# A hybrid attention and convolution block on eight cores: a rewrite of the whole kernel around 128-token interleaving, stationary P^T and merged stages

## The chip, the cores and the metric

The kernel runs on all 8 NeuronCores of one Trainium2 chip, two dies of four cores. The metric is the device time of the slowest core in microseconds. Engines are named as in the profile: PE is TensorE's matmul, PEld its weight load, DVE is VectorE, ACT is ScalarE, POOL is GpSimd, SP is SyncE. SP and POOL only issue DMAs here, apart from some POOL operations (the largest, in before, are eight of 2.4 us).

This program has a slower state that comes and goes: one die's cores, or both dies', show a lower granted TensorE clock and the run is some per cent longer. Before ran in 1544.24, 1740.64, 1663.52 and 1546.27 us; the first and last are fast runs. A ratio is the mean time of one kernel's fast runs over the mean of the other's fast runs of the same rounds, so it is not quite the ratio of the medians quoted beside it.

## The reference, cut to what matters

```python
D_MODEL, BATCH, SEQ = 1024, 4, 4096          # 4 differential heads, two 64-wide maps each, v of 128
xn = rmsnorm(x, norm_mix_g)
u = xn @ w_in                                # 5120 columns: conv b, c, v; q, k, v; two gates
y_a = (b_g * causal_conv3(c_g * v_a)) @ w_a_out
p = softmax(q k^T / 8 + alibi, causal)       # (B, H, 2, q, k)
o = (p[:, :, 0] - lam * p[:, :, 1]) @ v
y_b = (rmsnorm(o, subln_g) * (1 - lam_init)) @ w_b_out
x = x + (sigmoid(gate_a) * y_a + sigmoid(gate_b) * y_b) @ w_o
h = rmsnorm(x, norm_mlp_g) @ w_mlp_in        # 1024 -> 4096
x = x + square(relu(h)) @ w_mlp_out
return rmsnorm(x, norm_final_g)
```

Two cores share one batch element. Each owns half of its 4096 tokens and computes K and V for all of them.

## The kernel before

A core owns four blocks of 512 tokens. There are four stages, with a barrier of all engines between them: projections, attention, gates and output projection, MLP. In the first stage, normalising is done with tokens on partitions, where the scale is one number per partition, and the result is transposed on TensorE:

```python
S.op("act", lambda e: e.activation(xb[:ntok], xt[:ntok], AF.Square, accum_out=st[:ntok, 0:1]), ...)
... Ln, then Exp with scale -0.5: the reciprocal root ...
S.op("dve", lambda e: e.tensor_scalar_mul(xb[:ntok], xt[:ntok], st[:ntok, 2:3]), ...)
for c in range(8):
    S.op("pe", lambda e, c=c: e.transpose(pst[:, c, :ntok], xb[:ntok, c * 128:(c + 1) * 128], ...), ...)
S.op("dve", lambda e: e.tensor_tensor(dst, pst[:, :, :ntok], gcols...to_broadcast(...), ALU.mult), ...)
```

Attention keeps V stationary and streams P (keys on partitions, 512 queries). A second set of matmuls with an all-ones weight gives the row sums:

```python
mm(Ops[:, m, cs:512], Vt[:, kt, h * 128:(h + 1) * 128], PT[:, m, cs:512], ...)    # emit_pv
mm(Lps[:, m, cs:512], ones_bf, PT[:, m, cs:512], ...)                             # emit_lsum
```

In the MLP, W1 and W2 come in eight groups, each group's output is added to x in SBUF.

The softmax here doesn't subtract the row's maximum and nothing guards it: scores larger than these inputs give would overflow.

## Time and profile before

The page of the profiled run of before, slowest core. The first two lines are the span and each engine's busy time; the digits are tenths, in 40 equal slices, of PE busy, granted clock and DMA; the last line is the chain of work that ended last, by engine.

```profile
span 1546.6 us, 22141 instructions; the slowest of 8 cores (1531.8 to 1546.6 us)
...
PE 1376.5 (89%) x6824; PEld 584.5 (38%) x6824; DVE 709.2 (46%) x963; ACT 712.6 (46%) x1066; POOL 67.5 (4%) x72
...
PE   1989999878999999999367888897999999999995
...
PEclk9999999989999999999788999999999999999998
DMA  8861100330000000000197254443331313121105
...
PE 77%; DVE 8%; DMA 5%; ACT 5%; issue 3%; SPq 0%; POOL 0%; POOLq 0%; DVEq 0%; ACTq 0%
```

TensorE is busy 89% of the time and 77% of the last chain. The holes are at the start, around slice 19 (the hand-over from attention to gates) and at the very end. The table by stretches of the same core says what they are worth (columns: stretch, its length, then busy us and instruction count of each engine, clock, DMA share, GB/s):

```profile
core 7: us, PE busy (x) PEld busy (x) DVE busy (x) ACT busy (x) POOL busy (x), PEclk, DMA share, GB/s
0.00:65.00 65.00, 29.95 (x177) 15.84 (x178) 20.57 (x41) 21.02 (x48) 5.29 (x13) 1.00 0.80 161
...
362.00:760.00 398.00, 374.80 (x1888) 129.69 (x1886) 157.06 (x89) 309.93 (x308) 0.00 (x0) 0.99 0.00 1
760.00:820.00 60.00, 31.42 (x109) 11.51 (x108) 10.11 (x18) 21.25 (x39) 7.01 (x8) 0.73 0.97 201
820.00:1081.60 261.60, 223.81 (x1142) 104.40 (x1141) 126.80 (x195) 138.91 (x267) 22.80 (x27) 0.95 0.44 59
1081.60:1546.60 465.00, 445.65 (x2048) 200.19 (x2048) 240.63 (x408) 109.95 (x200) 30.01 (x22) 0.98 0.25 51
```

One step of attention, from the timeline of before in order of time (start us, duration us, engine, line; the x2 is a pair of 64-row QK matmuls, one in each half of the array's rows):

```profile
599.84 1.04 PE L348 MATMUL ps_all<-big 128*128 128x512 bf16 x4
600.01 1.11 ACT L675 ACTIVATE big<-ps_all,big 128x1024 bf16<-128x1024 f32 x1 [0.18 <-PE ps_all L350]
...
600.81 0.39 PE L350 MATMUL ps_all<-big 64*128 64x512 bf16 x2
...
601.13 1.04 PE L348 MATMUL ps_all<-big 128*128 128x512 bf16 x4
```

A step takes 1.29 us (599.84 to 601.13): four 512-column matmuls and a QK pair on TensorE, one 1.11 us exp on ACT. Attention is bound by TensorE, closely followed by the exps.

### The profile page before, as it was taken

The page shows a single profiled execution, that of the slowest core. Times are in us where ns is not written, and L with a number is a line of the kernel's source. Part 1 is how long each engine was busy: PE and PEld are TensorE (multiplying, and loading weights), DVE is VectorE, ACT ScalarE, POOL GpSimd, SP SyncE. Part 2 cuts the span into 40 slices and gives each one's busy share as a digit, 9 for nine tenths or more (in the row PEclk, how much of TensorE's full clock was granted, in tenths as well). Part 3 has the DMA queues.
Part 4 walks back from the last instruction along what each step waited for, and adds up shares of the span by engine and source line. Part 5 has one row for each costly group of instructions (what it writes and reads, how often), then busy time and mean ns, then how long its engine had stood idle before and what let it go on. Part 6 is the DMA issues. An engine that isn't in the chain of part 4 may idle for free.

```text
span 1546.6 us, 22141 instructions; the slowest of 8 cores (1531.8 to 1546.6 us)
## 1 busy us (share of the span) xinstructions
PE 1376.5 (89%) x6824; PEld 584.5 (38%) x6824; DVE 709.2 (46%) x963; ACT 712.6 (46%) x1066; POOL 67.5 (4%) x72
## 2 busy tenths in 40 slices
PE   1989999878999999999367888897999999999995
PEld 0444444323333333333123434343444444444441
DVE  2444454476553332333323454455253563564476
ACT  2553322356778878888244555463312112102217
POOL 0000000000000000000000000000000000000004
PEclk9999999989999999999788999999999999999998
DMA  8861100330000000000197254443331313121105
GB/s 163 182 159 53 44 28 1 54 56 1 1 1 1 1 1 1 1 0 1 19 259 103 36 74 53 57 56 55 53 57 31 53 29 55 28 32 25 28 11 208
DMA packets 63907, 80.06 MB, mean 52 GB/s; under 512 B 2984, under 2 KB 48168, under 8 KB 63792
## 3 DMA queue, kind: packets, MB, share of 16 engines
q0 software_dynamic: 53120, 44.04, 20.2%
q1 hardware_dynamic: 10672, 34.60, 7.0%
q8 instruction: 58, 0.95, 0.2%
q14 instruction: 57, 0.47, 0.1%
HBM read 114.29 MB, written 8.39 MB: 79 GB/s over the span
## 4 chain that ended last, share of the span: by engine, by line
PE 77%; DVE 8%; DMA 5%; ACT 5%; issue 3%; SPq 0%; POOL 0%; POOLq 0%; DVEq 0%; ACTq 0%
PE ps_all L348 70%; PE ps_all L350 6%; DMA big<-w_in 3%; DMA big<-xs 2%; DVE big L706 2%; DVE big L700 1%; DVE big L809 1%; ACT big L675 1%; ACT big L962 1%; ACT big L790 1%; PE ps_all L387 1%; PE ps_all L807 1%; ACT big L973 1%; DVE big L856 0%; DVE big L390 0%
## 5 line engine op out<-in xcount | busy, mean ns | idle before, releaser
L348 PE MATMUL ps_all<-big 128*128 128x512 bf16 (+3 forms) x5600 | 1270.6, 378 | 98.9 <-ACT big L834 24.4
L348 PEld LDWEIGHTS ps_all<-big 128*128 128x128 bf16 x5600 | 517.4, 100 | 741.2 <-issue 212.1
L675 ACT ACTIVATE big<-ps_all,big 128x1024 bf16<-128x1024 f32 (+1 forms) x320 | 329.1, 1049 | 101.2 <-PE ps_all L350 68.0
L997 ACT ACTIVATE big<-ps_all 128x512 bf16<-128x512 f32 x128 | 76.4, 597 | 319.1 <-PE ps_all L348 319.1
L1011 DVE TENSOR_TENSOR big<-ps_all,big 128x512 f32<-128x512 f32 x256 | 175.7, 690 | 39.3 <-PE ps_all L348 36.1
L350 PE MATMUL ps_all<-big 64*128 64x512 bf16 (+3 forms) x736 | 130.0, 350 | 11.6 <-ACT big L675 6.9
L998 DVE TENSOR_TENSOR big<-big 128x512 bf16<-128x512 bf16 x128 | 54.4, 425 | 175.9 <-ACT big L997 175.9
L706 DVE RECIPROCAL big<-big 128x1024 f32<-128x1024 f32 x16 | 104.8, 6552 | 2.0 <-DVE big L705 0.5
L700 DVE COPY big<-ps_all 128x1024 f32<-128x1024 f32 x16 | 19.6, 1222 | 175.5 <-PE ps_all L348 175.5
L350 PEld LDWEIGHTS ps_all<-big 64*128 64x128 bf16 x736 | 36.1, 93 | 147.6 <-issue 141.3
L850 DVE TENSOR_TENSOR big<-ps_all,big 128x512 f32<-128x512 f32 x32 | 22.1, 691 | 143.7 <-PE ps_all L348 94.1
L790 ACT ACTIVATE big<-big 128x1024 bf16<-128x1024 f32 x28 | 29.6, 1056 | 96.9 <-DVE big L789 91.3
L366 ACT ACTIVATE big<-big 128x1024 bf16<-128x1024 f32 (+1 forms) x33 | 34.9, 1058 | 56.9 <-DVE big L488 26.2
L319 POOL DMA_DIRECT2D big<-w_in x34 | 29.9, 883 | 710.3 <-DVE big L725 469.3
L387 PE MATMUL ps_all<-big 128*128 128x128 bf16 (+1 forms) x264 | 21.5, 228 | 39.4 <-DVE big L365 31.0
L376 DVE TENSOR_SCALAR big<-big 128x1024 bf16<-128x1024 f32 (+1 forms) x33 | 25.0, 759 | 53.1 <-ACT big L370 53.1
L390 DVE TENSOR_TENSOR big<-ps_all,big 128x1024 bf16<-128x1024 bf16 (+1 forms) x33 | 39.1, 1186 | 3.4 <-PE ps_all L387 3.3
L705 DVE COPY big<-ps_all 128x1024 f32<-128x1024 f32 x16 | 19.6, 1224 | 41.5 <-PE ps_all L348 41.4
L401 DVE CAST big<-ps_all 128x512 bf16<-128x512 f32 x24 | 16.5, 688 | 43.0 <-PE ps_all L348 43.0
L387 PEld LDWEIGHTS ps_all<-big 128*128 128x128 bf16 (+1 forms) x264 | 18.2, 102 | 47.1 <-issue 40.9
L725 DVE SCALAR_TENSOR_TENSOR big<-big 128x512 bf16<-128x512 f32 x16 | 12.0, 750 | 50.5 <-ACT big L724 50.5
L834 ACT ACTIVATE big<-ps_all,big 128x512 f32<-128x512 f32 x32 | 21.7, 679 | 27.3 <-PE ps_all L348 27.3
(67 smaller groups left out, 558.9 us busy)
## 6 DMA issues: line engine op xcount, KB each, us to landing
big<-xs SPq DMA_DIRECT2D x48, 512.0 KB, 7.8
big<-w_in POOLq DMA_DIRECT2D x32, 512.0 KB, 6.8
big<-w POOLq DMA_DIRECT2D x16, 1024.0 KB, 8.7
out<-big SPq DMA_DIRECT2D x16, 512.0 KB, 2.9
big<-w_in POOLq DMA_DIRECT2D x4, 1024.0 KB, 33.3
big<-w_in POOLq DMA_DIRECT2D x1, 2048.0 KB, 25.0
big<-w_o POOLq DMA_DIRECT2D x1, 2048.0 KB, 29.0
big<-w_a POOLq DMA_DIRECT2D x1, 1024.0 KB, 12.1
```

What stands on the lines that cost most here:

```text
L348: S.op("pe", lambda e: e.matmul(out, lhsT, rhs, start=start, stop=stop), reads=reads, writes=writes)
L350: S.op("pe", lambda e: e.matmul(out, lhsT, rhs, start=start, stop=stop, tile_position=tp), reads=reads, writes=writes)
L366: S.op("act", lambda e: e.activation(xb[:ntok], xt[:ntok], AF.Square, accum_out=st[:ntok, 0:1]), reads=[xkey, skey], writes=[xbkey, skey])
L387: S.op("pe", lambda e, c=c: e.transpose(pst[:, c, :ntok], xb[:ntok, c * 128:(c + 1) * 128], ident[:ntok, :ntok]), reads=[xbkey, "ident"], ...
L390: S.op("dve", lambda e: e.tensor_tensor(dst, pst[:, :, :ntok], gcols.unsqueeze(2).to_broadcast([128, 8, ntok]), ALU.mult), reads=[pkey, gk ...
L675: S.op("act", lambda e: e.activation(PT[:, :, cs:512], Sps[:, buf, :, cs:512], AF.Exp, bias=btab[:, bidx:bidx + 1], scale=0.125), reads=[" ...
L700: S.op("dve", lambda e: e.tensor_copy(c["Ocp"], Ops), reads=["O"], writes=[c["k"] + "O"])
L706: S.op("dve", lambda e: e.reciprocal(c["Lcp"], c["Lcp"]), reads=[k + "L"], writes=[k + "L"])
L790: S.op("act", lambda e: e.activation(xb, xt, AF.Square, accum_out=st[:, 0:1]), reads=[xkey, skey], writes=[xbkey, skey])
L997: S.op("act", lambda e, r=r, ph=ph: e.activation(r, ph, AF.Relu), reads=[phk], writes=[rk])
L998: S.op("dve", lambda e, r=r, fc=fc, sl=sl: e.tensor_tensor(hb[:, fc, sl * 512:(sl + 1) * 512], r, r, ALU.mult), reads=[rk], writes=["h2_%d ...
L1011: S.op("dve", lambda e, T=T, half=half, pz=pz: e.tensor_tensor(x_mid[:, T, half * 512:(half + 1) * 512], pz, x_mid[:, T, half * 512:(half ...
```

## The change: its intent and its core

The rewrite changes nearly every line; what matters of it is this.

1. Tokens are owned in interleaved tiles of 128, so that both cores' causal triangles are trimmed at 128 tokens.
2. P^T is the stationary operand and V the moving one, with a column of ones in V: one matmul gives 128 outputs and the row sum.
3. Attention is merged with projections of later blocks and with gates: between the halves of an attention step stand "chunks" of 4 or 8 matmuls, which all use one PSUM bank.
4. x arrives already transposed, so nothing of it is transposed on TensorE. But then a token's scale is needed along the free dimension, on all partitions. The kernel computes it with tokens on partitions from a second copy of x, writes the 512 numbers to DRAM and reads them back broadcast.
5. Intermediates (normalised x, branch inputs, residual x) are spilled to DRAM, and W1 and W2 stay resident in the MLP. The barriers are gone.

```diff
-            mm(Ops[:, m, cs:512], Vt[:, kt, h * 128:(h + 1) * 128], PT[:, m, cs:512], st["first"], st["last"],
-            mm(Lps[:, m, cs:512], ones_bf, PT[:, m, cs:512], st["first"], st["last"],
+                mm(oview(m, t), PT.ap[:, m, t * 128:(t + 1) * 128], v.ap[:, h, 0:129], start,
+                   p["last"] and s == 1, [PT, v], [pk(OB[(m, t)][0])], skip=True)
...
+    def stat_tile(blk, t, xt):
+        act(lambda e: e.activation(junk.ap, xt.ap, AF.Square, accum_out=ss1[blk].ap[:, t:t + 1]), ...)
+    def row_bcast(blk, src, dst, n, p):
+        row = rr_sp[blk, 0:n]                                   # in DRAM
+        ... dma_start(out=row.rearrange("(t p) -> p t", p=128), in_=src.ap[:, 0:4])
+        ld(dst.ap, ... rr_sp[blk:blk + 1, 0:n].partition_broadcast(128), [dst], [key])
...
+        def nrm(c):                                             # 8 of these per block, on DVE
+            dve(lambda e, k=k: e.scalar_tensor_tensor(x[k].ap, x[k].ap, ccol(C_GMIX + k), R_b.ap, ...))
...
+    def merged(g, upto, ratio):
+        oring[0] = Ring([7])                                    # one PSUM bank for all chunks
+        for slot in attn(g):
+            run_deferred()
+            credit += ratio / 2.0
+            while credit >= 1.0: ... one_chunk()
+        run_deferred(True)      # (called after it)
...
+    m_w1()                      # all of W1 and a quarter of W2, issued at once after attention
+    until(...)                  # the last two gate groups
+    m_load(0)                   # the first MLP block's input
```

## The prediction

> All times are for the fast state. (Before ran in 1544 to 1741 us; its profile, both dies near clock 0.96, took 1546.6.)
>
> What bounds before. The page shows PE busy 89% and 77% of the chain that ended last: TensorE, with holes. In the raw matmul records, back-to-back starts are 216 ns apart for 512 columns, 56 ns for 128 columns with a new weight each time (transposes), and a row-tiled QK pair adds about 420 ns between 512-column matmuls (312 before it, 322 to the next, less 216). With the built program's counts, before needs about 1324 us of warm PE. The other 222 us are holes: the table by stretches shows PE busy 30 of the first 65 us (DMA share 0.80), 57 of 71 us at the start of attention (clock 0.81; the 6.55 us reciprocals are in the chain), 31 of 60 us at 760-820 (waiting for w_in gate weights, DMA share 0.97), 224 of 262 us in the gate stage, 20 of 40 us at the end. The MLP is already solid.
>
> What the change does to PE. It removes 640 PV and 640 row-sum matmuls (about 253 us at 512-column pace) and puts in 2176 matmuls of 129 columns: about 122 us at the transposes' pace. The Trainium skill's "TensorE: Matmul & The Clock Gate", section "Back-to-back issue gap", gives about 81 ns for a load-and-multiply stream at N=128; this trace shows 56, and I use that (81 would cost 54 us more). 128-token interleaving makes both halves of the diagonal triangular, and four QK matmuls in a row pay one mode switch instead of two: QK 138 to 90 us. Pre-transposed x and no mask matmuls: 672 128-column matmuls become 192, 38 to 11 us. Projections, gates and MLP keep 4096 matmuls (884 us). Sum: about 1109 us, 215 less. PE is the chain, so all of it is critical.
>
> Holes after. Start: the first 4 blocks need some 30 MB; before's queues moved about 280 to 320 source-GB/s when full, so DMA still paces the first 100 us or so: 55 us lost. Attention merged with other chunks hides the exps (1.11 us each; 329 us in all) and gate weights, so the 760-820 hole and reciprocal stalls go. But merged chunks share one PSUM bank: each must be evacuated (0.6-0.7 us, sometimes behind two exps on ACT) before the next starts. Some 200 merged chunks at 0.2-0.5 us: 65 us. Head epilogues hold the O banks about 1 us x16. MLP hand-over and tail: 20 us. Tanh and exp should share a table ("ScalarE: Activation LUTs", "Table sets": tanh is listed with exp); before shows one load in all, 1.28 us.
>
> Predicted 1260 us, range 1190 to 1350: about 0.82 of before. Faster by over 2%: 0.96; within 2%: 0.02; slower: 0.02.
>
> Right if: 129-column starts 56-60 ns apart; PE over 90% busy; MLP still about 445 us; PE chain share above 85%; DVE busy far below 709 us (256 MLP accumulations at 0.69 us become 32); no idle hole over 10 us after the first 120 us. Wrong if: 129-column starts near 80-100 ns; many PE waits on ACT or DVE copies of the single bank; table loads recurring in the gate stage; PE waiting on xT or R after 120 us.
>
> Dangers: Pool's tiny pow operations queued behind its DMA issues, which would hold up DVE and then PE; DMA-bound start longer than estimated; a denser PE bringing a lower granted clock on all cores, so that no run is fast (then 1350 or more).

## The result

The changed kernel took 1753.73 us (median of 4 runs, 1750.18 to 1758.26) against 1544 to 1546 in fast runs of before: a ratio of 1.135 (1.131 to 1.138). It is correct, and 13.5% slower where 18% faster was predicted.

The page of the changed kernel, the same lines and, last, the chain by line of kernel.py:

```profile
span 1748.7 us, 20490 instructions; the slowest of 8 cores (1730.7 to 1748.7 us)
...
PE 1243.2 (71%) x7168; PEld 585.5 (33%) x7168; DVE 500.4 (29%) x1135; ACT 529.8 (30%) x744; POOL 61.6 (4%) x97
...
PE   3053255575746768785896986939439999999998
...
PEclk9576567677777889776798998979769999999999
DMA  8877210810312110724003014980760020120101
...
PE 58%; DMA 22%; DVE 10%; issue 4%; ACT 3%; POOL 1%; DVEq 0%; SPq 0%; ACTq 0%; POOLq 0%
PE ps_all L386 57%; DMA rr_sp<-big 6%; DMA big<-rr_sp 5%; DMA big<-xs 5%; ACT big L670 2%; DMA big<-x_sp 2%; DMA x_sp<-big 1%; DMA xm_sp<-big 1%; DVE big L706 1%; DVE big L489 1%; DMA big<-xn_sp 1%; DVE big L830 1%; DVE big L710 1%; DMA big<-ya_sp 1%; DVE big L814 1%
```

TensorE does less (1243 us busy against 1377) and waits more: 505 us of the span (1748.7 less 1243.2) against 170. DMA has gone from 5% to 22% of the chain, and half of that is `rr_sp`, the 2 KB row of scales going to DRAM and back. After the first four slices (175 us) and up to the loads before the MLP, the DMA digits are mostly 0 to 3 where TensorE has holes: there, DMAs are waited for without a full queue. In the first four slices DMA is at 7 to 8, so the page alone can't tell a late row from a queue full of bytes; r1 below can. The clock row is 5 to 7 in most slices in which TensorE has holes.

The table by stretches of the changed kernel:

```profile
60.00:330.00 270.00, 122.68 (x657) 54.01 (x657) 83.91 (x217) 45.93 (x74) 13.66 (x19) 0.69 0.46 63
...
797.00:1090.00 293.00, 223.79 (x1612) 111.83 (x1611) 93.58 (x214) 138.69 (x168) 6.93 (x10) 0.87 0.22 67
1090.00:1297.00 207.00, 121.67 (x576) 54.62 (x575) 59.53 (x85) 31.18 (x48) 3.49 (x7) 0.80 0.69 149
1297.00:1748.70 451.70, 443.78 (x2048) 200.65 (x2048) 100.12 (x192) 94.46 (x160) 8.69 (x16) 0.99 0.13 45
```

The MLP is as solid as it was (444 us for its 2048 matmuls, 451.7 us in all, before 465). Everything is lost in front of it: in 270 us from 60 on TensorE is busy for 123, and 207 us before the MLP for 122.

What the DVE and PE stood idle for, from the changed kernel's waits (us in total, times, longest); the first line is of DVE, the other four of PE:

```profile
DVE big L489 <- DMA big<-rr_sp: 171.4, 7, 34.9
...
PE ps_all L386 <- DVE big L564: 66.4, 8, 32.7
PE ps_all L386 <- DVE big L706: 60.4, 12, 21.4
PE ps_all L386 <- DMA big<-x_sp: 49.1, 1, 49.1
PE ps_all L386 <- DVE big L489: 46.5, 3, 45.1
```

L564 is the copy of a Q chunk from PSUM, 0.7 us of work. It is blamed for 66 us because it stood in DVE's queue behind L489, the normalisation, and L489 stood before the scale row. Two instances, in the changed kernel's timeline of DVE and, in the last line, of PE: L549 evacuates V chunks, the bracket is idle time and its releaser.

```profile
55.19 1.41 DVE L549 TENSOR_SCALAR big<-ps_all,big 128x512 bf16<-128x512 f32 x2
85.59 2.74 DVE L489 SCALAR_TENSOR_TENSOR big<-big 128x512 bf16<-128x512 bf16 x4 [28.99 <-DMA big<-rr_sp]
88.24 0.74 DVE L549 TENSOR_SCALAR big<-ps_all,big 128x512 bf16<-128x512 f32 x1
...
144.06 1.41 DVE L489 SCALAR_TENSOR_TENSOR big<-big 128x512 bf16<-128x512 bf16 x2 [34.88 <-DMA big<-rr_sp]
145.40 0.68 DVE L564 CAST big<-ps_all 128x512 bf16<-128x512 f32 x1
...
146.23 0.58 PE L386 MATMUL ps_all<-big 64*128 64x512 bf16 x1 [32.67 <-DVE big L564]
```

In the first, DVE stops for 29 us in front of an 0.7 us operation, and the next V evacuation, for which all data is there (TensorE had done its matmuls by 41.4 us), stands behind it. TensorE itself waits here for the normalised x. In the second, TensorE waits 32.67 us for a copy of Q that stands behind a normalisation of another block. The chain of work at the first place, in order of time (start, us, what):

```profile
41.12 12.63 DMA big<-xs
53.83 1.16 ACT big L430 x2
55.40 1.05 POOL big L426
56.52 13.82 DMA rr_sp<-big
70.41 15.02 DMA big<-rr_sp
...
86.92 1.41 DVE big L489 x2
```

Load x, square it, take the root, 13.8 us to write 2 KB, 15 us to read it back, and only then normalise: this chain runs once for each of seven blocks. Neither bytes nor a full queue explain the whole of the write's time: those issued at 203, 492 and 620 us landed after 14.0, 8.2 and 8.4 us, although their 4-byte packets had all started within 1.4 us and this core's DMA engines were busy for about a tenth of that time at most. What fills the rest of the time to landing, the trace doesn't show. Over the whole trace, 166 us of TensorE's idle time overlap a DVE wait for that row, and another 50 us overlap an ACT wait for the second copy of x alone (both worked out from the start times in the trace).

The matmuls themselves are what the prediction expected. The groups of the changed kernel by form (busy us, mean ns of one; mean is latency, not pace):

```profile
L386 PE MATMUL ps_all<-big 128*128 128x129 bf16 x2176 | 182.2, 236 | 61.7 <-DVE big L706 60.4 <-DVE big L697 0.2 <-DVE big L675 0.2
...
L430 ACT ACT_TABLE_LOAD x1 | 1.3, 1283 | 17.1 <-DMA big<-xs 17.1
```

In the raw records two consecutive 129-column matmuls start 57 ns apart at the median. The table is loaded once, so tanh between exps costs no reload; "ScalarE: Activation LUTs" of the Trainium skill, section "Table sets: the hidden batching unit", lists both in one set, and the trace agrees (1.28 us, once).

The time can be added up. Warm need is the sum of matmul paces from the prediction; beyond need is the rest of PE's busy time; idle is span less PE busy:

| slowest core | warm need | beyond need | idle | span | us at half clock |
|---|---|---|---|---|---|
| before | 1324 | 52 | 170 | 1546.6 | 120 |
| predicted | 1109 | not counted | 151 | 1260 | |
| changed | 1109 | 134 | 505 | 1748.7 | 491 |

"TensorE: Matmul & The Clock Gate", section "Part 1: The HAM clock gate (the "warmup" mystery)", says that an idle window of about 3.4 us puts the array at half clock. The clock records agree: on this core of the changed kernel each of the 28 holes of 3 us or more after the first 30 us overlaps a half-clock stretch or is followed by one within 1.1 us, no such stretch is shorter than 3.41 us, and there are 491 us of them against 120 before. So a hole costs more than its length. A third level, 0.81, appears for 215 us on this core and not at all on cores 4 and 5, whose spans of 1730.7 and 1736.8 us are about 1% shorter; it isn't the main cause. An estimate of what the clock cost, from PE's busy time at each level: 146 us at half clock lose 73, and 184 us at 0.81 lose 35. That is 108 of the 134 us beyond need, and 35 of the 52 in before. The rest is not explained.

### The profile page after: what moved, and what is told of

Its sections match the earlier page's. It is cut to its first block, busy times and chain, and to the rows that moved or that the text cites. A ratio compares the mean times of both kernels' runs of the same rounds, so it can differ in the third digit from the quotient of the medians.

```text
span 1748.7 us, 20490 instructions; the slowest of 8 cores (1730.7 to 1748.7 us)
## 1 busy us (share of the span) xinstructions
PE 1243.2 (71%) x7168; PEld 585.5 (33%) x7168; DVE 500.4 (29%) x1135; ACT 529.8 (30%) x744; POOL 61.6 (4%) x97
## 4 chain that ended last, share of the span: by engine, by line
PE 58%; DMA 22%; DVE 10%; issue 4%; ACT 3%; POOL 1%; DVEq 0%; SPq 0%; ACTq 0%; POOLq 0%
PE ps_all L386 57%; DMA rr_sp<-big 6%; DMA big<-rr_sp 5%; DMA big<-xs 5%; ACT big L670 2%; DMA big<-x_sp 2%; DMA x_sp<-big 1%; DMA xm_sp<-big 1%; DVE big L706 1%; DVE big L489 1%; DMA big<-xn_sp 1%; DVE big L830 1%; DVE big L710 1%; DMA big<-ya_sp 1%; DVE big L814 1%
## 5 line engine op out<-in xcount | busy, mean ns | idle before, releaser
L386 PE MATMUL ps_all<-big 128*128 128x512 bf16 (+4 forms) x6976 | 1229.5, 344 | 424.5 <-DVE big L564 66.4
L386 PEld LDWEIGHTS ps_all<-big 128*128 128x128 bf16 (+1 forms) x6976 | 573.8, 102 | 1074.5 <-issue 674.5
L670 ACT ACTIVATE big<-ps_all,big 128x1024 bf16<-128x1024 f32 (+3 forms) x384 | 320.2, 880 | 356.9 <-PE ps_all L386 340.0
L791 DVE SCALAR_TENSOR_TENSOR big<-big,ps_all 128x512 f32<-128x512 f32 x64 | 44.0, 688 | 190.0 <-PE ps_all L386 189.9
L780 ACT ACTIVATE big<-ps_all,big 128x512 f32<-128x512 f32 x64 | 44.0, 687 | 154.7 <-PE ps_all L386 154.7
L489 DVE SCALAR_TENSOR_TENSOR big<-big 128x512 bf16<-128x512 bf16 x56 | 39.2, 745 | 171.4 <-DMA big<-rr_sp 171.4
L915 ACT ACTIVATE big<-big 128x1024 bf16<-128x1024 f32 x16 | 16.9, 1057 | 208.3 <-DVE big L910 208.3
L430 ACT ACTIVATE big<-big 128x1024 bf16<-128x1024 f32 x32 | 33.8, 1057 | 129.1 <-DMA big<-xs 129.1
L910 DVE SCALAR_TENSOR_TENSOR big<-ps_all,big 128x512 f32<-128x512 f32 x32 | 24.0, 751 | 163.2 <-PE ps_all L386 163.2
L818 ACT ACTIVATE big<-big 128x1024 bf16<-128x1024 f32 x16 | 16.9, 1057 | 81.2 <-DVE big L814 81.2
L675 DVE TENSOR_TENSOR big<-big 128x256 bf16<-128x256 bf16 x64 | 18.6, 290 | 73.6 <-ACT big L670 73.5
L814 DVE SCALAR_TENSOR_TENSOR big<-ps_all,big 128x512 f32<-128x512 f32 x32 | 22.1, 689 | 59.1 <-PE ps_all L386 35.0
L605 DVE TENSOR_TENSOR big<-ps_all,big 128x512 f32<-128x512 f32 x16 | 11.1, 692 | 87.5 <-PE ps_all L386 74.0
L537 DVE CAST big<-ps_all 128x512 bf16<-128x512 f32 x32 | 21.8, 690 | 46.4 <-PE ps_all L386 46.4
L554 DVE CAST big<-ps_all 128x512 bf16<-128x512 f32 x28 | 19.4, 691 | 29.7 <-PE ps_all L386 29.5
```

What stands on the lines that cost most here:

```text
L386: S.op("pe", lambda e: e.matmul(out, lhsT, rhs, start=start, stop=stop, skip_group_check=skip), reads, writes)
L430: act(lambda e: e.activation(junk.ap, xt.ap, AF.Square, accum_out=ss1[blk].ap[:, t:t + 1]), [xt], [junk, ss1[blk]])
L489: dve(lambda e, k=k: e.scalar_tensor_tensor(x[k].ap, x[k].ap, ccol(C_GMIX + k), R_b.ap, ALU.mult, ALU.mult), [x[k], cst, R_b], [x[k]])
L537: dve(lambda e: e.tensor_copy(dst.ap, ps), [key], [dst])
L670: act(lambda e, a=a, b=b, c=c, s=s, PT=PT, scale=scale: e.activation(PT.ap[:, :, a:b], Sb[s][:, :, a:b], AF.Exp, bias=ccol(C_BTAB + c), sc ...
L780: act(lambda e: e.activation(t.ap, ps, AF.Tanh, bias=hbg.ap[:, 8 * w + dm:8 * w + dm + 1], scale=0.5), [key, hbg], [t])
```

## The experiments

Theory A: the scale row's round trip through DRAM holds DVE's queue, which the timeline above shows to be worked off in order, and TensorE behind it. Rivals: B, the start is bound by bytes; C, merging through one PSUM bank costs more than it gains.

Fast means below are of 2 to 4 runs each. The runs stand in four groups, each with fast runs of before between 1544 and 1552 us on the same chip, so differences between kernels of different groups are good to a few us.

### r1_onchip: the scale row by a matmul

```diff
-        S.dma("sp", w, [src], [key])                            # scales to DRAM
-        ld(dst.ap, ... rr_sp[blk:blk + 1, 0:n].partition_broadcast(128), [dst], [key])
+        for t in range(n // p):                                 # a diagonal matrix of the scales
+            dve(lambda e, t=t: e.tensor_scalar_mul(dg.ap[:p, t, 0:p], ident[:p, 0:p], src.ap[:p, t:t + 1]), ...)
+        for t in range(n // p):                                 # ones^T @ diag: every partition has the row
+            mm(ps[:, t * p:(t + 1) * p], ones32.ap[:p, :], dg.ap[:p, t, 0:p], True, True, ...)
+        dve(lambda e: e.tensor_copy(dst.ap, ps[:, 0:n]), [key], [dst])
```

> The row of per-token scales reaches all partitions through a 128-column fp32 matmul of ones with a diagonal matrix instead of two DMAs through DRAM; same result as the changed kernel. Theory A (the DRAM round trip of some 30 us per block holds up VectorE's in-order queue, and TensorE behind it): in the changed kernel's trace 166 of 497 us of TensorE idle time overlap a VectorE wait for that row, and the array runs at half clock for a while after each hole, so 1560 us, 1510 to 1620. Rival B (the start is bound by the bytes loaded, the round trip only fills the same time): within 2% of 1752, because the loads are the same. Rival C (chunks merged through one PSUM bank): within 3% of 1752.

Measured: correct, fast mean 1580.3 us, 1.021 of before (1.019 to 1.023); the changed kernel was 1.135. That is 174 us less than its fast mean of 1754.0, what theory A said. Its page:

```profile
span 1582.1 us, 20633 instructions; the slowest of 8 cores (1563.4 to 1582.1 us)
...
PE 1222.3 (77%) x7226; PEld 584.6 (37%) x7226; DVE 513.5 (32%) x1172; ACT 529.5 (33%) x744; POOL 61.7 (4%) x98
```

Idle fell from 505 to 360 us and half clock from 491 to 329. The two profiled spans differ by 167 us: 146 are idle time, 21 PE busy time (by the same estimate the clock cost 72 us here, 36 less, and the new matmuls take some of that back). Rivals B and C both said no change and are out as the main cause.

### r2_unread: the round trip kept, but nobody waits for it

```diff
-                dve(... e.scalar_tensor_tensor(x[k].ap, x[k].ap, ccol(C_GMIX + k), R_b.ap, ...), [x[k], cst, R_b], ...)
+                dve(... e.scalar_tensor_tensor(x[k].ap, x[k].ap, ccol(C_GMIX + k), R_c.ap, ...), [x[k], cst, R_c], ...)
```

> Wrong result on purpose: the round trip's DMAs are all issued as in the changed kernel, but the normalisation reads a constant row, so that VectorE doesn't wait for them. Theory A in its narrow form (VectorE's wait is what costs): about 1580 us, like the on-chip version. If instead the cost is the in-order SyncE queue, whose later loads of x stand behind the round trip (its waits for the scale row sum to some 180 us in the trace), then it stays above 1680 us.

Measured: wrong result; fast mean 1629 us from two fast runs, 9 us apart, 1.053 (1.048 to 1.058). That lies between the two expectations, 1580 and above 1680. So about 125 of the 174 us are DVE's wait for the seven blocks' rows. The other 49 us may come from the round trip's other half. SP issues it in order, and behind its wait stand the loads of x; ACT's waits for x in this trace are still as large as in the changed kernel:

```profile
ACT big L432 <- DMA big<-xs: 133.3, 19, 37.9
```

That much of the 49 us are those waits fits: 84 us of TensorE idle overlap an ACT wait for x here, 57 in r1. Another 9 us overlap a DVE wait for the scale row of the convolution's halo (the 32 tokens in front of the tiles), which this edit left in place. But no run took SP's queue away alone, so this part is not shown.

### r3_early: the first MLP input loaded earlier

```diff
     m_w1()
+    m_load(0)
     until(...)
-    m_load(0)
```

> The load of the first MLP block's input is issued before the last two gate groups instead of after them; nothing else changes. The changed kernel's trace has one TensorE hole of 49 us there. Expected 1752 minus 45 to 60, about 1700 us, if that load is late only because it is issued late and shares the queues with 12 MB of W2; within 1% of 1752 if TensorE would have waited for the weights anyway.

Measured: correct, fast mean 1707 us (two fast runs), 1.103: 47 us less, as expected. TensorE was really waiting for that 1 MB load, which had been issued in the company of 12 MB of weights.

### r4_nomerge and r7_onchip_nomerge: what merging is worth

```diff
-        _NC_CACHE["nc"] = build_program()
+        _NC_CACHE["nc"] = build_program(merge=False)
```

> Attention is not merged with projections and gates (the chunks run before and after it, with eight PSUM banks). Theory A: merging is not the fault; the holes of the round trip remain and the exps are no longer hidden behind chunks, so 1780 to 1900 us. Rival C (the single PSUM bank that merged chunks share, and the in-order ACT and DVE queues that they share with the exps, cost more than merging gains): clearly faster than 1752, 1600 to 1700 us.

> The on-chip row version without merging: what merging attention with the chunks is worth once the round trip is gone. With it in place merging gained only 1.8% (1785 against 1752). If merging hides the exps as it is meant to: 1581 plus 60 to 130 us, since 320 us of exps on ACT then stand against some 215 us of QK and PV; if its single PSUM bank takes back what it gains: 1581 within 2%.

Measured: 1787 us without merging when the round trip is there (1.155, so merging gained some 33 us), and 1656 us without merging when it is gone (1.069, so merging gained 75 us over r1). Rival C falls twice: merging pays, and the round trip had eaten half of its gain. PE waits on the evacuation of chunks exist: in r1 they add up to about 53 us, in 74 waits (the V copy, 12.6 us in all, is the largest), where the prediction had put 65 us. No run gave the merged chunks a second bank, so what the single bank alone costs is not shown.

### r5_handover: order of the loads at the stage changes

```diff
+    w1_at = {(2, 1): 1, (2, 3): 2, ... (3, 7): 8}      # W1 group g may load when gate (i, dm) is done
-    m_w1()
+    w1_load(0, ())
+    m_load(0)
...
-            out.append((0, lambda: g_loads(nxt)))
+            out.append((0, lambda: (g_loads(nxt), g_loads2(nxt))))
...
     def g_w1():
+        g_loads(0)                                     # normalised x of gate group 0, before its weights
```

> On the on-chip row version (1581 us), the loads at the stage changes are put in better order, result unchanged: early load of the first MLP input; the normalised x and branch inputs of a gate group loaded one group ahead, into a slot that is free earlier; the nine W1/W2 loads released one by one by the progress of the gate groups instead of all at once. Theory A2 (late and crowded DMAs at the stage changes make holes): the on-chip trace has holes of 49 (MLP input), 20 (normalised x), 25 (x for the residual) and 10 us (branch inputs), so 1581 minus 95 to 110, about 1480 us. If only the MLP input was real and the others are made up by other waits: about 1530.

Measured: correct, 1537.6 us, 0.9925 (0.990 to 0.995). Only 43 us of the 95 to 110 came. The two theories of the expectation are both off: the MLP input's hole went, and two of the others moved. The waits of TensorE in r5:

```profile
PE ps_all L841 <- DVE big L830: 31.6, 6, 13.6
PE ps_all L387 <- DMA big<-ya_sp: 28.7, 1, 28.7
```

The branch inputs (`ya_sp`) now waited behind the gate weights where the normalised x had waited. The transposes (L841) waited, behind the copy in front of them, for residual loads and stores that ran beside W1 loads; that sum was 32.2 us in r1 and is unchanged.

### r6_noflush: the deferred epilogue isn't forced out

```diff
         merged(g, names[end], ratio)
-        run_deferred(True)
...
+    until(done[0] + 6)
+    run_deferred(True)
     w1_load(0, ())
```

> As the hand-over version, and the last head's second epilogue half of each attention group is no longer forced out right away but comes four chunks later, as for other heads. The on-chip trace shows TensorE at the four forced transposes waiting 37 us in all. Expected 30 to 40 us below the hand-over version, about 1445 us; if the epilogue's VectorE work is the limit and not the place of the transposes, within 10 us of it.

Measured: correct, 1519.3 us, 0.981: 18 us less, half of what was expected. The four waits at those transposes (8 to 10 us each in r1) shrank to 3.4 us or less each, but not all of that reached the end.

### r8_pace: the order changed once more

```diff
-    w1_at = {(2, 1): 1, (2, 3): 2, (2, 5): 3, (2, 7): 4, (3, 1): 5, (3, 3): 6, (3, 5): 7, (3, 7): 8}
+    w1_at = {(2, 1): 1, (2, 2): 2, (2, 3): 3, (2, 4): 4, (3, 0): 5, (3, 1): 6, (3, 2): 7, (3, 3): 8}
...
-        cload(W2[q]..., [W2[q]])
+        cload(W2[q]..., [W2[q]], ["tz15"])              # after the last residual
...
+    W += [(0, g_w1)] + cv[:6] + [(0, lambda: g_loads2(0))] + cv[6:] + [(0, g_w2)]
```

> As the no-flush version (1519 us), with three places of the DMA order changed again: the first gate group's branch inputs are loaded six chunks earlier, the W1/W2 loads are released in the gate chunks and kept out of the stretches where the residual x is loaded and stored, the last three W2 loads wait for the last residual. The hand-over version gained 43 us of 100 because two holes only moved: 30 us waiting for branch inputs behind gate weights, and 31 us at the transposes waiting for x behind weight loads. If both are a matter of order: about 1465 us. If the bytes themselves don't fit the time there: within 15 us of 1519.

Measured: correct, 1468.5 us, 0.949 of before (0.946 to 0.953): 51 us less, as expected. This is a version that beats both kernels, 5% faster than before. Its page:

```profile
span 1469.1 us, 20642 instructions; the slowest of 8 cores (1447.3 to 1469.1 us)
...
PE 1213.0 (83%) x7226; PEld 582.3 (40%) x7226; DVE 511.9 (35%) x1172; ACT 530.2 (36%) x744; POOL 61.7 (4%) x98
```

Its waits of PE, the four largest:

```profile
PE ps_all L387 <- DVE big L454: 43.5, 4, 21.9
PE ps_all L387 <- DVE big L711: 42.0, 12, 7.7
PE ps_all L387 <- ACT big L675: 25.1, 36, 2.3
PE ps_all L387 <- DVE big L949: 24.9, 4, 11.2
```

L454 and L949 are the start (the first blocks' scales and their raw x), L711 the heads' epilogues that hold the output banks, L675 the exps.

### r9_xs4 and r11_xs_quarter: what binds the start

```diff
-    xtok = Ring([ar.take("xtok%d" % k, [1024], F32) for k in range(2)])
+    xs4 = ar.take("xs4", [4, 1024], BF16)               # r9: a block's token-major x in one load, a block ahead
...
-        cload(xs4.ap, xs_d[blk * 512:(blk + 1) * 512, :].rearrange(...), [xs4])
+        cload(xs4.ap[:, :, 0:256], xs_d[blk * 512:(blk + 1) * 512, 0:256].rearrange(...), [xs4])   # r11
```

> As r8, and the token-major x, needed only for its row sums of squares, comes as one bf16 tile of 512 tokens per block, loaded right after the block before has been squared, instead of four fp32 tiles through two buffers just in time. Theory: ACT's in-order queue stands before those loads while exps wait behind them (57 us of TensorE idle overlap an ACT wait for x in the no-flush version, and part of the first 100 us), so 40 to 70 us below r8, about 1410. If the start is bound by bytes: less than 15 us below r8, as the bytes from DRAM are the same.

> Wrong result on purpose: r9 with the row sums of squares taken from a quarter of the columns, so 12 MB less of x comes from DRAM before attention ends (and each square on ACT is 0.6 us shorter). r9 gained nothing over r8, against the theory of ACT's queue. If the start is bound by bytes instead (14 MB have landed when the second block can start, at 59 us): the first block's hole shrinks by 8 to 12 us and the whole by 20 to 35 us, about 1440. If neither bytes nor ACT's wait bind: within 8 us of 1467.

Measured: r9 is correct, 1466.4 us, 0.948: no gain over r8. My theory that ACT's in-order wait for x was worth 40 to 70 us falls; r9 also moved these loads from SP's queue to POOL's, and in its trace ACT's wait for the second block's x ends at 59.7 us, 5 us later than in r8 (54.7), though TensorE's idle time under ACT's waits for x fell from 56 to 44 us. r11, wrong, took 1451.2 us, 0.939: 15 us less than r9, between the two expectations. Nearly all of it is the start: of the first 100 us TensorE idles 44, against 58 in r9 and 57 in r8. So bytes matter at the start, but taking 3 of the first 14 MB away leaves most of that idle time; and r11 also shortens ACT's squares. What binds the start beyond that stays open.

### r10_pv_twice: what the new PV matmuls cost where they stand

```diff
                 mm(oview(m, t), PT.ap[...], v.ap[:, h, 0:129], start, False, ...)
+                mm(oview(m, t), PT.ap[...], v.ap[:, h, 0:129], False, p["last"] and s == 1, ...)
```

> r8 with every 129-column PV matmul issued twice (sums and row sums both double, so the result is the same). It measures what those 2176 matmuls cost where they stand. If they cost the 56 to 57 ns that the prediction took and are on the critical path: r8's 1469 plus 124 us, 1580 to 1605. If short matmuls with a new weight each cost 81 to 100 ns in the merged stream: plus 176 to 218 us, 1645 to 1690. If they only fill holes: less than plus 60.

Measured: correct, 1530.8 us, 0.989: 62 us more than r8 for 2176 more matmuls. The page of r10:

```profile
span 1534.0 us, 24994 instructions; the slowest of 8 cores (1509.9 to 1534.0 us)
...
PE 1330.5 (87%) x9402; PEld 713.0 (46%) x9402; DVE 512.5 (33%) x1172; ACT 530.5 (35%) x744; POOL 61.7 (4%) x98
```

PE is busy 117 us more (1330.5 against 1213.0) and idle 52 us less (203.5 against 256.1). So a PV matmul costs the 57 ns that the prediction took (57 ns from start to start here too), not 81 to 100, but only half of that time is on the critical path even in the mended kernel. The result lies between the first expectation and the last, next to the last (under 60). (Two cores of this profile, the slowest among them, had 0.81 clock for about 120 us; the other six are 54 us longer than in r8 on average, so 62 is rather too much than too little, and that the matmuls only fill holes is not excluded.)

## Why the prediction was wrong, point by point

**The array's need: right.** 129-column matmuls follow each other at 57 ns, the exps' table is not reloaded, the MLP takes 444 us of PE, DVE is busy 500 us instead of 709. PE busy fell, as forecast, though by 133 instead of 215 us, mostly because a larger part of it ran at a lower clock (by the estimate above 108 us lost against 35).

**"Holes after": the step that failed.** The prediction left 151 us for them (1260 less 1109; its terms sum to 156); they were 505. It gave 55 us to the start, which it put down to bytes, 65 us to the single bank, 16 us to the heads' epilogues, 20 us to hand-over and tail. The scale row's round trip, which none of these contains, is 174 us by r1, and TensorE waited for it: 166 us of its idle time lie under DVE's waits for the row. It is the largest part of the miss that a run took away, not all of it: of the 494 us between the prediction and the changed kernel's fast mean, the row is 174, the order of loads and epilogues in r5, r6 and r8 another 112, and 209 remain. The start's 55 us were about right in size (TensorE idles 58 of the first 100 us in r1, 71 in the changed kernel), but r11 puts only some 14 of them down to the bytes that it took away. The prediction had the pieces: it saw the diff's `row_bcast`, and it named "PE waiting on xT or R after 120 us" as a sign of being wrong, but it priced the bytes of the start and never the latency of a DRAM write followed by a DRAM read, seven times, in front of an in-order DVE queue. Before's list of DMAs has tiny ones, of 0.5 to 32 KB, that took 2 to 10 us to land at the start; nothing in it is like 14 plus 15 us, but it might have been asked.

**Hand-over, 20 us: mis-sized.** r3, r5 and r8 changed the order of loads at the stage changes and took 47 us (r3, off the changed kernel) and 43 plus 51 us (r5 and r8). The prediction counted neither that the intermediates now go through DRAM at every stage change, nor that weights issued all at once stand in front of them.

**The single bank, 65 us: about right, as far as the waits tell.** PE's waits on chunk evacuations in r1 are about 53 us, and r4 and r7 show merging gaining 33 and 75 us in spite of them.

**Heads' epilogues, 16 us: mis-sized.** In r1 TensorE waits 42.0 us for the epilogues that hold the output banks (L711 there) and 36.8 us at the four forced transposes, which r6 moved.

**The clock: left out.** PE was busy for 134 us beyond the warm need, where before had 52; of the 134, half-clock stretches after holes are 73 and the 0.81 level 35, by the estimate above.

**"PE is the chain, so all of it is critical": wrong for the new kernel.** In before, PE was 77% of the chain; in the changed kernel 58%. r10 measures it: 117 us more PE work cost 62 us even in r8.

**The dangers.** POOL's pow behind its DMA issues was named first and is not what happened; the pow in the chain above takes 1.05 us. A longer start did happen. A lower clock on all cores came, but mostly as half clock after holes; the densest stage, the MLP, ran at 0.99.

What stays open: r8 still idles 256 us and has 104 us of PE busy time beyond the need (some 61 of them slow clock, by the same estimate), so it is 209 us above the predicted 1260. About 57 us of the idle time lie in the first 100 us, about 40 us are epilogues holding the output banks; the rest is spread over waits of a few us each, which no run took apart.

## What to carry to other kernels

Before a rewrite is priced by the busiest engine's work, list every value that one in-order queue waits for, and follow each back to its source: a 2 KB row that takes a way through DRAM, once for each of seven blocks, cost 174 us, and a dozen lines that keep it on the chip gave it back. When a load is late, look at what was issued with it and before it on the same queue before asking for more bandwidth; holes that are mended in one place reappear at the next load in line until the order as a whole is right. Doubling a suspected cost (here the PV matmuls, whose doubling leaves the result as it was) tells how much of it is on the critical path, which no busy percentage does.

## What the Trainium skill lacked or had wrong

- "TensorE: Matmul & The Clock Gate", section "Back-to-back issue gap": gives about 81 ns per matmul for a sustained stream of load and multiply at N=128. Here 129 columns with a new weight each time follow at 57 ns (median of 1956 pairs in the changed kernel, 4132 in r10), and 128-column transposes at 56 ns.
- "TensorE: Matmul & The Clock Gate", section "Part 1: The HAM clock gate (the "warmup" mystery)": advises to budget the 13/16 clock for sustained dense matmul on all cores. Here all eight cores ran the MLP's 2048 matmuls densely at the same time (from 1300 to 1735 us of the changed kernel's fast profile, PE was busy 423 to 435 us of 435 on each) at a granted clock of 0.99 to 1.00; 0.81 appeared on six cores, for 97 to 226 us, before the MLP. The slow runs, in which it may hold, left no trace.
- "DMA: Bandwidth & Descriptors", section "Anatomy of one DMA — SWDGE (gpsimd) path": fits 2.0 us plus bytes over bandwidth for DMAs issued by GpSimd; the row's DMAs are issued by SyncE. A 2 KB write to DRAM of 4-byte elements landed in 14.0 us (median of 7; 8 to 21 us), its read back as 256 KB in 15.0 us (median of 7; 6 to 21 us); the 32-element write took 4.0 us. Three of the writes took 8 to 14 us with this core's DMA engines nearly idle. I found no page with the landing time of such a write of many small elements, nor of the round trip.
- "TensorEngine Tiling (Array Packing)", "Key Properties": says that switching the tiling mode drains the array, without a number. Here the switch into a 64-row pair takes 312 ns after a 512-column matmul instead of 216, and 322 ns pass from the pair to the next: a pair costs about 420 ns, hardly less than two 512-column matmuls in a row (432).
